# Writing y over x in six large buffers, with all transfers in a fixed order on one hardware queue

## The chip, the cores and the metric

The kernel runs on one NeuronCore of a Trainium2 chip. The metric is the time of one execution in microseconds (us), measured on the device. Every time is a median of several executions; a result is called faster or slower than the kernel before when it is clear of 2%. Smaller differences between variants are read only where the four executions of one lie apart from those of the other. Executions over 1.5% above the fastest of their kernel count as slow; ratios leave them out. Profiles come from one execution each. The "span" of a profile runs from the core's first to its last instruction; where a run lists both for one execution, the time is 1.7 to 2.2 us longer.

## The reference

```python
x: (16, 2048, 256) float32      # 32,768 rows of 1 KB
W: (256, 256);  lora_A: (256, 16);  lora_B: (16, 256);  lora_E: (16,)

y = x_flat @ W
y = y + scale * (((x_flat @ lora_A) * lora_E) @ lora_B)
```

The low-rank part can be folded into the weights, so that y = x @ weff. What remains is to read 33.55 MB of x, multiply by one 256x256 matrix and write 33.55 MB of y.

## The kernel before

Both kernels compute in the same way, two sub-rows of 128 at a time: TensorE (PE) transposes x in float32, ScalarE (ACT) casts the result to bf16, PE multiplies, VectorE (DVE) copies the product from PSUM into SBUF. What differs is where x and y lie and how the transfers are queued.

```python
CFG = dict(B_SZ=16,                       # 16 rows of 1 KB per partition: 2 MB tiles
    FIRST=[(2, [1, 1], [1, 1]), (6, [2, 4], [2, 4]), (8, [4, 4], [4, 4])],
    LAST=[(8, [4, 4], [4, 4]), (8, [8], [4, 4])],
    X_BUFS=3, Y_BUFS=3, NONSTEADY_BUFS=2, OUT_ENGINE="gpsimd", ...)   # cut

def load_x(it):                           # x tile: one of 3 buffers
    x_tile = xpool.tile([P, bsz, K], FP32, tag=f"x_{bsz}", ...)       # cut
    nc.sync.dma_start(out=x_tile[:, s:s + sz, :], in_=x_ap(it, s, s + sz))
...
for it in range(n_iters):
    y_tile = ypool.tile([P, bsz, M], FP32, tag=f"y_{bsz}", ...)       # one of 3 buffers
    for g in range(bsz // CG):
        # PE transposes -> nc.scalar.copy(out=xt, in_=psum_xt) -> PE matmuls   (cut)
        nc.vector.tensor_copy(out=y_tile[:, g * CG:(g + 1) * CG, :], in_=psum_y)
        # when a piece is complete:
        out_eng.dma_start(out=out_ap(it, s, e), in_=y_tile[:, s:e, :])
    load_x(it + 1)
```

Loads go through SyncE's hardware queue, stores through the software queue of GpSimd (POOL). A load waits until PE has read the x tile that it overwrites; DVE waits until the y tile that it overwrites has been stored.

Of the kernel before, what the change touches and what calls it, by code (L numbers as in the profile page):

```python
# [1 line left out]

# [5 lines left out]


CFG = dict(
    B_SZ=16,
    CG=2,
    IN_SPLIT=1,
    OUT_SPLIT=1,
    FIRST=[(2, [1, 1], [1, 1]), (6, [2, 4], [2, 4]), (8, [4, 4], [4, 4])],
    LAST=[(8, [4, 4], [4, 4]), (8, [8], [4, 4])],
    X_BUFS=3,
    Y_BUFS=3,
    XT_BUFS=8,  # L20
    PS_XT_BUFS=3,
    PS_Y_BUFS=3,
    NONSTEADY_BUFS=2,
    OUT_ENGINE="gpsimd",
    SETUP_ENGINE="gpsimd",
)


@with_exitstack
def kernel(  # L30
    ctx: ExitStack,
    tc: tile.TileContext,
    x: bass.AP,
    W: bass.AP,
    lora_A: bass.AP,
    lora_B: bass.AP,
    lora_E: bass.AP,
    scale: bass.AP,
    out: bass.AP,
):  # L40
    nc = tc.nc
    P = 128
    FP32 = mybir.dt.float32
    BF16 = mybir.dt.bfloat16

    CG = CFG["CG"]
    X_BUFS = CFG["X_BUFS"]
    Y_BUFS = CFG["Y_BUFS"]
    XT_BUFS = CFG["XT_BUFS"]
    PS_XT_BUFS = CFG["PS_XT_BUFS"]  # L50
    PS_Y_BUFS = CFG["PS_Y_BUFS"]

    out_eng = getattr(nc, CFG["OUT_ENGINE"])
    setup_eng = getattr(nc, CFG["SETUP_ENGINE"])

    x_flat = x.flatten_outer_dims()
    out_flat = out.flatten_outer_dims()
    N, K = x_flat.shape
    M = out_flat.shape[1]
    R = lora_B.shape[0]  # L60
    KC = K // P

    n_sub_total = N // P
    plan = []
    first = CFG["FIRST"] or []
    last = CFG["LAST"] or []
    nfirst = sum(p[0] for p in first)
    nlast = sum(p[0] for p in last)
    B_SZ = CFG["B_SZ"]
    n_mid = (n_sub_total - nfirst - nlast) // B_SZ  # L70
    assert n_mid * B_SZ + nfirst + nlast == n_sub_total, "sizes must tile exactly"
    isp = B_SZ // CFG["IN_SPLIT"]
    osp = B_SZ // CFG["OUT_SPLIT"]
    plan.extend(first)
    plan.extend([(B_SZ, [isp] * CFG["IN_SPLIT"], [osp] * CFG["OUT_SPLIT"])] * n_mid)
    plan.extend(last)
    for bsz, ip, op in plan:
        assert sum(ip) == bsz and sum(op) == bsz and bsz % CG == 0

    const = ctx.enter_context(tc.tile_pool(name="const", bufs=1))  # L80
    setup = ctx.enter_context(tc.tile_pool(name="setup", bufs=1))
    ps_setup = ctx.enter_context(tc.tile_pool(name="ps_setup", bufs=1, space=bass.MemoryType.PSUM))
    xpool = ctx.enter_context(tc.tile_pool(name="xpool", bufs=X_BUFS))
    ypool = ctx.enter_context(tc.tile_pool(name="ypool", bufs=Y_BUFS))
    xTpool = ctx.enter_context(tc.tile_pool(name="xTpool", bufs=XT_BUFS))
    ps_xT = ctx.enter_context(tc.tile_pool(name="ps_xT", bufs=PS_XT_BUFS, space=bass.MemoryType.PSUM))
    ps_y = ctx.enter_context(tc.tile_pool(name="ps_y", bufs=PS_Y_BUFS, space=bass.MemoryType.PSUM))

    row_offs = []
    acc = 0  # L90
    for bsz, _, _ in plan:
        row_offs.append(acc)
        acc += bsz * P

    def x_ap(it, s0, s1):
        bsz = plan[it][0]
        r0 = row_offs[it]
        return (
            x_flat[r0:r0 + bsz * P, :]
            .rearrange("(p b) k -> p b k", b=bsz)[:, s0:s1, :]  # L100
        )

    def out_ap(it, s0, s1):
        bsz = plan[it][0]
        r0 = row_offs[it]
        return (
            out_flat[r0:r0 + bsz * P, :]
            .rearrange("(p b) m -> p b m", b=bsz)[:, s0:s1, :]
        )

    x_tiles = {}

    steady_b = CFG["B_SZ"]

    def load_x(it):
        bsz, in_pieces, _ = plan[it]
        x_tile = xpool.tile(
            [P, bsz, K], FP32, name=f"x_tile_{bsz}", tag=f"x_{bsz}",
            bufs=X_BUFS if bsz == steady_b else CFG["NONSTEADY_BUFS"],
        )  # L120
        s = 0
        for sz in in_pieces:
            nc.sync.dma_start(out=x_tile[:, s:s + sz, :], in_=x_ap(it, s, s + sz))
            s += sz
        x_tiles[it] = x_tile

    load_x(0)

    ident = const.tile([P, P], FP32)
    make_identity(nc, ident)  # L130

    a_sb = setup.tile([P, KC, R], FP32)
    setup_eng.dma_start(out=a_sb, in_=lora_A.rearrange("(c p) r -> p c r", p=P))  # L133
    e_sb = setup.tile([R, 1], FP32)
    setup_eng.dma_start(out=e_sb, in_=lora_E[:, None])  # L135
    b_bf = setup.tile([R, M], BF16)
    nc.gpsimd.dma_start(out=b_bf, in_=lora_B)  # L137
    w_sb = setup.tile([P, KC, M], FP32)
    for c in range(KC):
        setup_eng.dma_start(out=w_sb[:, c, :], in_=W[c * P:(c + 1) * P, :])  # L140

    ps_at = ps_setup.tile([R, KC, P], FP32, name="ps_at")
    for c in range(KC):
        nc.tensor.transpose(ps_at[:, c, :], a_sb[:, c, :], ident)
    ate = setup.tile([R, KC, P], BF16)
    nc.vector.tensor_scalar(
        out=ate,
        in0=ps_at,
        scalar1=e_sb,
        scalar2=float(scale),  # L150
        op0=mybir.AluOpType.mult,
        op1=mybir.AluOpType.mult,
    )
    ps_aeb = ps_setup.tile([P, KC, M], FP32, name="ps_aeb")
    for c in range(KC):
        nc.tensor.matmul(ps_aeb[:, c, :], ate[:, c, :], b_bf, start=True, stop=True)
    weff = const.tile([P, KC, M], BF16)
    nc.vector.tensor_add(out=weff, in0=w_sb, in1=ps_aeb)  # L158

    n_iters = len(plan)  # L160
    for it in range(n_iters):
        if it not in x_tiles:
            load_x(it)
        x_tile = x_tiles.pop(it)
        bsz, _, out_pieces = plan[it]

        y_tile = ypool.tile(
            [P, bsz, M], FP32, name=f"y_tile_{bsz}", tag=f"y_{bsz}",
            bufs=Y_BUFS if bsz == steady_b else CFG["NONSTEADY_BUFS"],
        )  # L170

        bounds = []
        acc2 = 0
        for sz in out_pieces:
            acc2 += sz
            bounds.append(acc2)

        piece_idx = 0
        piece_start = 0
        for g in range(bsz // CG):  # L180
            psum_xt = ps_xT.tile([P, CG, KC, P], FP32, name="psum_xt")
            xt = xTpool.tile([P, CG, KC, P], BF16, name="xt")
            psum_y = ps_y.tile([P, CG, M], FP32, name="psum_y")
            for j in range(CG):
                sb = g * CG + j
                for c in range(KC):
                    nc.tensor.transpose(  # L187
                        psum_xt[:, j, c, :],
                        x_tile[:, sb, c * P:(c + 1) * P],
                        ident,  # L190
                    )
            nc.scalar.copy(out=xt, in_=psum_xt)  # L192
            for j in range(CG):
                for c in range(KC):
                    nc.tensor.matmul(  # L195
                        psum_y[:, j, :],
                        xt[:, j, c, :],
                        weff[:, c, :],
                        start=(c == 0),
                        stop=(c == KC - 1),  # L200
                    )
            nc.vector.tensor_copy(out=y_tile[:, g * CG:(g + 1) * CG, :], in_=psum_y)  # L202

            done = (g + 1) * CG
            while piece_idx < len(bounds) and bounds[piece_idx] <= done:
                e = bounds[piece_idx]
                s = piece_start
                out_eng.dma_start(out=out_ap(it, s, e), in_=y_tile[:, s:e, :])  # L208
                piece_start = e
                piece_idx += 1  # L210

        if it + 1 < n_iters:
            load_x(it + 1)


# [1 line left out]
_INS = ['x', 'W', 'lora_A', 'lora_B', 'lora_E', 'scale']  # L217
_OUTS = [((16, 2048, 256), 'float32')]
#: Inputs that are plain numbers.
_NUMBERS = {'scale': 1.0}  # L220


# [26 lines left out]
```

## Time and profile before

| | before |
|---|---|
| time, median (range) | 171.93 us (170.65 to 172.49) |
| span of the profile | 169.2 us |
| bytes moved, mean rate over the span | 67.55 MB, 399 GB/s |
| PE busy | 79% |

First the page of the profiled execution. Each digit is the busy share, in tenths, of one of 40 slices; PEclk is the granted PE clock, DMA the mean of the 16 DMA engines.

```profile
span 169.2 us, 2603 instructions
...
PE 134.2 (79%) x1028; PEld 104.1 (62%) x1028; DVE 84.0 (50%) x130; ACT 71.0 (42%) x129; POOL 16.5 (10%) x35
...
PE   0679999999961599962999999998969696999810
...
PEclk9999999999998589996599999999999999999975
DMA  5999999999999999999999999999999999994992
GB/s 121 310 446 430 425 408 381 435 440 422 428 419 433 440 409 438 432 420 434 430 422 434 434 430 422 426 434 434 426 434 432 434 430 422 387 426 167 379 387 108
DMA packets 6715, 67.55 MB, mean 399 GB/s; under 512 B 848, under 2 KB 1136, under 8 KB 2992
```

DMA is full almost throughout, PE is not. The rate has two weak places, the first two slices and the last four. Next, the table by stretch: start and end, length, then busy time of PE, weight loads, DVE, ACT and POOL (with counts), the granted clock, the DMA share and GB/s.

```profile
0.00:12.00 12.00, 5.53 (x24) 4.60 (x25) 0.93 (x2) 3.63 (x5) 3.64 (x11) 1.00 0.83 286
12.00:152.50 140.50, 120.35 (x941) 93.57 (x940) 76.81 (x120) 62.61 (x116) 10.16 (x19) 0.95 1.00 425
152.50:157.50 5.00, 4.77 (x41) 3.58 (x38) 3.00 (x5) 3.05 (x6) 1.07 (x2) 1.00 0.47 193
157.50:162.50 5.00, 3.53 (x29) 2.39 (x26) 3.20 (x5) 1.73 (x4) 1.07 (x2) 1.00 0.99 406
162.50:169.20 6.70, 0.00 (x0) 0.00 (x0) 0.07 (x1) 0.00 (x0) 0.53 (x1) 0.53 0.53 208
```

Look at the third row: DMA share 0.47 while PE is busy 4.77 of 5.00 us. The DMA has run out of work, and for this once PE is what everybody waits for. The timeline of POOL says what it waits for (start, duration, what, and in brackets how long POOL stood idle before and what ended it):

```profile
146.27 0.53 POOL L208 DMA_DIRECT2D out_dram<-y_tile_1523  x1 [9.19 <-DVE y_tile_1523 L202]
154.67 0.53 POOL L208 DMA_DIRECT2D out_dram<-y_tile_1631  x1 [7.87 <-DVE y_tile_1631 L202]
...
162.87 0.53 POOL L208 DMA_DIRECT2D out_dram<-y_tile_1797  x1 [1.51 <-DVE y_tile_1797 L202]
```

All loads have landed by then (the last 2 MB load was issued at 123.2 us and took 20.7), and the stores come only as fast as PE finishes tiles. In the table of waits (who waited for whom, us in total, times, longest):

```profile
PE psum_xt L187 <- DMA x_tile_657<-in_x_dram: 5.3, 1, 5.3
PE psum_xt L187 <- DMA x_tile_873<-in_x_dram: 4.6, 1, 4.6
...
DVE y_tile_551 L202 <- DMA out_dram<-y_tile_227: 3.3, 1, 3.3
```

An idle PE costs nothing at that moment, because DMA was full (436 GB/s from 52 to 58 us).

### The profile page before, as it was taken

The page shows a single profiled execution, that of the slowest core. Times are in us where ns is not written, and L with a number is a line of the kernel's source. Part 1 is how long each engine was busy: PE and PEld are TensorE (multiplying, and loading weights), DVE is VectorE, ACT ScalarE, POOL GpSimd, SP SyncE. Part 2 cuts the span into 40 slices and gives each one's busy share as a digit, 9 for nine tenths or more (in the row PEclk, how much of TensorE's full clock was granted, in tenths as well). Part 3 has the DMA queues.
Part 4 walks back from the last instruction along what each step waited for, and adds up shares of the span by engine and source line. Part 5 has one row for each costly group of instructions (what it writes and reads, how often), then busy time and mean ns, then how long its engine had stood idle before and what let it go on. Part 6 is the DMA issues. An engine that isn't in the chain of part 4 may idle for free.

```text
span 169.2 us, 2603 instructions
## 1 busy us (share of the span) xinstructions
PE 134.2 (79%) x1028; PEld 104.1 (62%) x1028; DVE 84.0 (50%) x130; ACT 71.0 (42%) x129; POOL 16.5 (10%) x35
## 2 busy tenths in 40 slices
PE   0679999999961599962999999998969696999810
PEld 0568777777741477742877777776757474777600
DVE  0027666666273066660366666665647366466620
ACT  3242555555541145530355555555535453355500
POOL 7005201010100010100101010101000010101220
PEclk9999999999998589996599999999999999999975
DMA  5999999999999999999999999999999999994992
GB/s 121 310 446 430 425 408 381 435 440 422 428 419 433 440 409 438 432 420 434 430 422 434 434 430 422 426 434 434 426 434 432 434 430 422 387 426 167 379 387 108
DMA packets 6715, 67.55 MB, mean 399 GB/s; under 512 B 848, under 2 KB 1136, under 8 KB 2992
## 3 DMA queue, kind: packets, MB, share of 16 engines
q0 software_dynamic: 3392, 33.84, 47.8%
q1 hardware_dynamic: 3312, 33.56, 47.6%
q8 instruction: 8, 0.13, 0.3%
q14 instruction: 3, 0.02, 0.0%
HBM read 33.85 MB, written 33.55 MB: 398 GB/s over the span
## 4 chain that ended last, share of the span: by engine, by line
issue 81%; POOL 9%; DMA 4%; DVE 1%; POOLq 1%; PE 0%; DVEq 0%
POOL out_dram L208 7%; DMA w_sb<-in_W_dram 4%; POOL a_sb L133 1%; PE psum_y L195 0%; DVE y_tile_106 L202 0%; DVE weff L158 0%; POOLq L244 0%; POOL w_sb L140 0%; POOL b_bf L137 0%; POOL e_sb L135 0%; POOLq L208 0%; POOL ident masks.py:199 0%; POOL ident masks.py:197 0%; POOLq masks.py:199 0%; DVEq L158 0%
## 5 line engine op out<-in xcount | busy, mean ns | idle before, releaser
L192 ACT CAST xt<-psum_xt 128x512 bf16<-128x512 f32 x128 | 69.7, 588 | 89.4 <-PE psum_xt L187 89.4
L195 PE MATMUL psum_y<-weff,xt 128*128 128x256 bf16 x512 | 72.6, 280 | 6.6 <-DVE y_tile_551 L202 1.4
L195 PEld LDWEIGHTS <-xt 128*128 128x128 bf16 x512 | 42.0, 100 | 33.5 <-ACT xt L192 27.3
L202 DVE COPY y_tile_551<-psum_y 128x512 f32<-128x512 f32 x8 | 5.1, 685 | 10.9 <-PE psum_y L195 7.6
L187 PE MATMUL psum_xt<-ident,x_tile_873 128*128 128x128 f32 x32 | 5.9, 338 | 4.6 <-DMA x_tile_873<-in_x_dram 4.6
L202 DVE COPY y_tile_767<-psum_y 128x512 f32<-128x512 f32 x8 | 5.2, 686 | 8.7 <-PE psum_y L195 8.7
L187 PE MATMUL psum_xt<-ident,x_tile_657 128*128 128x128 f32 x32 | 5.3, 315 | 5.3 <-DMA x_tile_657<-in_x_dram 5.3
L187 PEld LDWEIGHTS psum_xt<-ident,x_tile_657 128*128 128x128 f32 x32 | 4.5, 168 | 5.6 <-issue 5.5
L187 PEld LDWEIGHTS psum_xt<-ident,x_tile_873 128*128 128x128 f32 x32 | 4.9, 179 | 5.0 <-issue 4.9
L202 DVE COPY y_tile_1415<-psum_y 128x512 f32<-128x512 f32 x8 | 5.2, 688 | 4.5 <-PE psum_y L195 3.8
L202 DVE COPY y_tile_1523<-psum_y 128x512 f32<-128x512 f32 x8 | 5.2, 688 | 4.5 <-PE psum_y L195 3.8
L202 DVE COPY y_tile_1307<-psum_y 128x512 f32<-128x512 f32 x8 | 5.2, 688 | 4.5 <-PE psum_y L195 4.1
L202 DVE COPY y_tile_875<-psum_y 128x512 f32<-128x512 f32 x8 | 5.3, 688 | 3.9 <-PE psum_y L195 3.9
L202 DVE COPY y_tile_659<-psum_y 128x512 f32<-128x512 f32 x8 | 5.2, 688 | 3.5 <-PE psum_y L195 3.5
L202 DVE COPY y_tile_1199<-psum_y 128x512 f32<-128x512 f32 x8 | 5.2, 686 | 3.5 <-PE psum_y L195 3.5
L202 DVE COPY y_tile_1631<-psum_y 128x512 f32<-128x512 f32 x8 | 5.3, 688 | 3.2 <-PE psum_y L195 3.2
L202 DVE COPY y_tile_227<-psum_y 128x512 f32<-128x512 f32 x8 | 5.2, 686 | 3.1 <-PE psum_y L195 3.1
L202 DVE COPY y_tile_983<-psum_y 128x512 f32<-128x512 f32 x8 | 5.2, 686 | 3.0 <-PE psum_y L195 3.0
L202 DVE COPY y_tile_443<-psum_y 128x512 f32<-128x512 f32 x8 | 5.2, 686 | 3.0 <-PE psum_y L195 3.0
L202 DVE COPY y_tile_335<-psum_y 128x512 f32<-128x512 f32 x8 | 5.2, 686 | 3.0 <-PE psum_y L195 3.0
L202 DVE COPY y_tile_1091<-psum_y 128x512 f32<-128x512 f32 x8 | 5.2, 687 | 3.0 <-PE psum_y L195 3.0
L187 PE MATMUL psum_xt<-ident,x_tile_1521 128*128 128x128 f32 x32 | 4.3, 273 | 1.4 <-DMA x_tile_1521<-in_x_dram 1.4
(74 smaller groups left out, 143.1 us busy)
## 6 DMA issues: line engine op xcount, KB each, us to landing
x_tile_225<-in_x_dram SPq DMA_DIRECT2D x1, 2048.0 KB, 12.2
x_tile_333<-in_x_dram SPq DMA_DIRECT2D x1, 2048.0 KB, 16.9
x_tile_441<-in_x_dram SPq DMA_DIRECT2D x1, 2048.0 KB, 23.9
x_tile_549<-in_x_dram SPq DMA_DIRECT2D x1, 2048.0 KB, 14.0
out_dram<-y_tile_227 POOLq DMA_DIRECT2D x1, 2048.0 KB, 19.3
x_tile_657<-in_x_dram SPq DMA_DIRECT2D x1, 2048.0 KB, 23.0
out_dram<-y_tile_335 POOLq DMA_DIRECT2D x1, 2048.0 KB, 17.7
x_tile_765<-in_x_dram SPq DMA_DIRECT2D x1, 2048.0 KB, 22.1
```

Source lines behind the costliest of these rows:

```text
L133: setup_eng.dma_start(out=a_sb, in_=lora_A.rearrange("(c p) r -> p c r", p=P))
L187: nc.tensor.transpose(psum_xt[:, j, c, :], x_tile[:, sb, c * P:(c + 1) * P], ident,)
L192: nc.scalar.copy(out=xt, in_=psum_xt)
L195: nc.tensor.matmul(psum_y[:, j, :], xt[:, j, c, :], weff[:, c, :], start=(c == 0), stop=(c == KC - 1),)
L202: nc.vector.tensor_copy(out=y_tile[:, g * CG:(g + 1) * CG, :], in_=psum_y)
L208: out_eng.dma_start(out=out_ap(it, s, e), in_=y_tile[:, s:e, :])
```

## The change

The intent is one unbroken stream of transfers: SBUF is laid out as six buffers of one 4 MB chunk each (192 KB per partition, where the x and y tiles of before took 160 KB), y takes the place of x, and one queue carries loads and stores in a written order, loads first, so that PE is fed early and stores are always queued. Rows become 32 KB per partition. Setup tensors go on the same queue. The rest (transposes, cast, matmuls, copies) is unchanged, except that the small weight product is now in float32 and the cast has six buffers in place of eight.

```diff
-    B_SZ=16, X_BUFS=3, Y_BUFS=3, OUT_ENGINE="gpsimd", ...
+ROWS = 32
+N_CHUNKS = 8
+N_HOMES = 6
+LOAD_PIECES = {0: [8, 8, 16]}
+ORDER = [
+    "L0", "L1", "L2", "L3", "L4", "L5",
+    "S0", "S1", "L6", "S2", "L7", "S3", "S4", "S5", "S6", "S7",
+]
...
+    homes = [homes_pool.tile([P, ROWS, K], FP32, name=f"home{h}", ...) for h in range(N_HOMES)]
+    def load(c, s, e):
+        nc.sync.dma_start(out=homes[c % N_HOMES][:, s:e, :], in_=x_chunks[c, :, s:e, :])
+    def store(c, s, e):
+        nc.sync.dma_start(out=y_chunks[c, :, s:e, :], in_=homes[c % N_HOMES][:, s:e, :])
...
-            nc.vector.tensor_copy(out=y_tile[:, g * CG:(g + 1) * CG, :], in_=psum_y)
+            nc.vector.tensor_copy(out=home[:, g * CG:(g + 1) * CG, :], in_=psum_y)
...
+    done = -1
+    for step in ORDER:
+        c = int(step[1:])
+        if step[0] == "L":
+            if c:
+                for s, e in pieces(c):
+                    load(c, s, e)
+        else:
+            while done < c:
+                done += 1
+                compute(done)
+            store(c, 0, ROWS)
```

More of the change, by code (lines that the diff above doesn't have):

```diff
@@ L5 @@
 import concourse.tile as tile
-from concourse import bass_utils, mybir
+from concourse import mybir
 from concourse.masks import make_identity
 from concourse._compat import with_exitstack
-CFG = dict(
-    B_SZ=16,
-    CG=2,
-    IN_SPLIT=1,
-    OUT_SPLIT=1,
-    FIRST=[(2, [1, 1], [1, 1]), (6, [2, 4], [2, 4]), (8, [4, 4], [4, 4])],
-    LAST=[(8, [4, 4], [4, 4]), (8, [8], [4, 4])],
-    X_BUFS=3,
-    Y_BUFS=3,
-    XT_BUFS=8,
-    PS_XT_BUFS=3,
-    PS_Y_BUFS=3,
-    NONSTEADY_BUFS=2,
-    OUT_ENGINE="gpsimd",
-    SETUP_ENGINE="gpsimd",
-)
+P = 128
+FP32 = mybir.dt.float32
+BF16 = mybir.dt.bfloat16
+ROWS = 32
[6 more added lines that the diff above has]
+]
+CG = 2
 @with_exitstack
@@ L41 @@
     nc = tc.nc
-    P = 128
-    FP32 = mybir.dt.float32
-    BF16 = mybir.dt.bfloat16
-    CG = CFG["CG"]
-    X_BUFS = CFG["X_BUFS"]
-    Y_BUFS = CFG["Y_BUFS"]
-    XT_BUFS = CFG["XT_BUFS"]
-    PS_XT_BUFS = CFG["PS_XT_BUFS"]
-    PS_Y_BUFS = CFG["PS_Y_BUFS"]
-    out_eng = getattr(nc, CFG["OUT_ENGINE"])
-    setup_eng = getattr(nc, CFG["SETUP_ENGINE"])
     x_flat = x.flatten_outer_dims()
@@ L61 @@
     KC = K // P
-    n_sub_total = N // P
-    plan = []
-    first = CFG["FIRST"] or []
-    last = CFG["LAST"] or []
-    nfirst = sum(p[0] for p in first)
-    nlast = sum(p[0] for p in last)
-    B_SZ = CFG["B_SZ"]
-    n_mid = (n_sub_total - nfirst - nlast) // B_SZ
-    assert n_mid * B_SZ + nfirst + nlast == n_sub_total, "sizes must tile exactly"
-    isp = B_SZ // CFG["IN_SPLIT"]
-    osp = B_SZ // CFG["OUT_SPLIT"]
-    plan.extend(first)
-    plan.extend([(B_SZ, [isp] * CFG["IN_SPLIT"], [osp] * CFG["OUT_SPLIT"])] * n_mid)
@@ L76 @@
-    plan.extend(last)
-    for bsz, ip, op in plan:
-        assert sum(ip) == bsz and sum(op) == bsz and bsz % CG == 0
+    assert N == N_CHUNKS * ROWS * P and K == M
     const = ctx.enter_context(tc.tile_pool(name="const", bufs=1))
-    setup = ctx.enter_context(tc.tile_pool(name="setup", bufs=1))
+    homes_pool = ctx.enter_context(tc.tile_pool(name="homes", bufs=1))
+    xTpool = ctx.enter_context(tc.tile_pool(name="xTpool", bufs=6))
     ps_setup = ctx.enter_context(tc.tile_pool(name="ps_setup", bufs=1, space=bass.MemoryType.PSUM))
-    xpool = ctx.enter_context(tc.tile_pool(name="xpool", bufs=X_BUFS))
@@ L84 @@
-    ypool = ctx.enter_context(tc.tile_pool(name="ypool", bufs=Y_BUFS))
-    xTpool = ctx.enter_context(tc.tile_pool(name="xTpool", bufs=XT_BUFS))
-    ps_xT = ctx.enter_context(tc.tile_pool(name="ps_xT", bufs=PS_XT_BUFS, space=bass.MemoryType.PSUM))
-    ps_y = ctx.enter_context(tc.tile_pool(name="ps_y", bufs=PS_Y_BUFS, space=bass.MemoryType.PSUM))
-    row_offs = []
-    acc = 0
-    for bsz, _, _ in plan:
-        row_offs.append(acc)
-        acc += bsz * P
-    def x_ap(it, s0, s1):
-        bsz = plan[it][0]
-        r0 = row_offs[it]
-        return (
-            x_flat[r0:r0 + bsz * P, :]
-            .rearrange("(p b) k -> p b k", b=bsz)[:, s0:s1, :]
-        )
@@ L103, in out_ap @@
-    def out_ap(it, s0, s1):
-        bsz = plan[it][0]
-        r0 = row_offs[it]
-        return (
-            out_flat[r0:r0 + bsz * P, :]
-            .rearrange("(p b) m -> p b m", b=bsz)[:, s0:s1, :]
-        )
-    x_tiles = {}
-    steady_b = CFG["B_SZ"]
-    def load_x(it):
-        bsz, in_pieces, _ = plan[it]
-        x_tile = xpool.tile(
-            [P, bsz, K], FP32, name=f"x_tile_{bsz}", tag=f"x_{bsz}",
-            bufs=X_BUFS if bsz == steady_b else CFG["NONSTEADY_BUFS"],
-        )
-        s = 0
-        for sz in in_pieces:
-            nc.sync.dma_start(out=x_tile[:, s:s + sz, :], in_=x_ap(it, s, s + sz))
-            s += sz
-        x_tiles[it] = x_tile
@@ L127 @@
-    load_x(0)
+    ps_xT = ctx.enter_context(tc.tile_pool(name="ps_xT", bufs=3, space=bass.MemoryType.PSUM))
+    ps_y = ctx.enter_context(tc.tile_pool(name="ps_y", bufs=3, space=bass.MemoryType.PSUM))
+    x_chunks = x_flat.rearrange("(c p b) k -> c p b k", p=P, b=ROWS)
+    y_chunks = out_flat.rearrange("(c p b) m -> c p b m", p=P, b=ROWS)
+    homes = [
+        homes_pool.tile([P, ROWS, K], FP32, name=f"home{h}", tag=f"home{h}")
+        for h in range(N_HOMES)
+    ]
+    def load(c, s, e):
+        nc.sync.dma_start(out=homes[c % N_HOMES][:, s:e, :], in_=x_chunks[c, :, s:e, :])
@@ new lines, in store, with pieces @@
+    def store(c, s, e):
+        nc.sync.dma_start(out=y_chunks[c, :, s:e, :], in_=homes[c % N_HOMES][:, s:e, :])
+    def pieces(c):
+        s = 0
+        for n in LOAD_PIECES.get(c, [ROWS]):
+            yield s, s + n
+            s += n
+    first = list(pieces(0))
+    load(0, *first[0])
+    w_sb = const.tile([P, KC, M], FP32)
+    nc.sync.dma_start(out=w_sb, in_=W.rearrange("(c p) m -> p c m", p=P))
+    a_sb = const.tile([P, KC, R], FP32)
+    nc.sync.dma_start(out=a_sb, in_=lora_A.rearrange("(c p) r -> p c r", p=P))
@@ L129 @@
+    e_sb = const.tile([R, 1], FP32)
+    nc.sync.dma_start(out=e_sb, in_=lora_E[:, None])
+    b_sb = const.tile([R, M], FP32)
+    nc.sync.dma_start(out=b_sb, in_=lora_B)
+    for s, e in first[1:]:
+        load(0, s, e)
     ident = const.tile([P, P], FP32)
     make_identity(nc, ident)
-    a_sb = setup.tile([P, KC, R], FP32)
-    setup_eng.dma_start(out=a_sb, in_=lora_A.rearrange("(c p) r -> p c r", p=P))
-    e_sb = setup.tile([R, 1], FP32)
-    setup_eng.dma_start(out=e_sb, in_=lora_E[:, None])
@@ L136 @@
-    b_bf = setup.tile([R, M], BF16)
-    nc.gpsimd.dma_start(out=b_bf, in_=lora_B)
-    w_sb = setup.tile([P, KC, M], FP32)
-    for c in range(KC):
-        setup_eng.dma_start(out=w_sb[:, c, :], in_=W[c * P:(c + 1) * P, :])
     ps_at = ps_setup.tile([R, KC, P], FP32, name="ps_at")
@@ L144 @@
         nc.tensor.transpose(ps_at[:, c, :], a_sb[:, c, :], ident)
-    ate = setup.tile([R, KC, P], BF16)
+    ate = const.tile([R, KC, P], FP32)
     nc.vector.tensor_scalar(
@@ L155, with compute @@
     for c in range(KC):
-        nc.tensor.matmul(ps_aeb[:, c, :], ate[:, c, :], b_bf, start=True, stop=True)
+        nc.tensor.matmul(ps_aeb[:, c, :], ate[:, c, :], b_sb, start=True, stop=True)
     weff = const.tile([P, KC, M], BF16)
     nc.vector.tensor_add(out=weff, in0=w_sb, in1=ps_aeb)
-    n_iters = len(plan)
-    for it in range(n_iters):
-        if it not in x_tiles:
-            load_x(it)
-        x_tile = x_tiles.pop(it)
-        bsz, _, out_pieces = plan[it]
-        y_tile = ypool.tile(
-            [P, bsz, M], FP32, name=f"y_tile_{bsz}", tag=f"y_{bsz}",
-            bufs=Y_BUFS if bsz == steady_b else CFG["NONSTEADY_BUFS"],
-        )
-        bounds = []
-        acc2 = 0
-        for sz in out_pieces:
-            acc2 += sz
-            bounds.append(acc2)
-        piece_idx = 0
-        piece_start = 0
-        for g in range(bsz // CG):
+    def compute(c):
+        home = homes[c % N_HOMES]
+        for g in range(ROWS // CG):
             psum_xt = ps_xT.tile([P, CG, KC, P], FP32, name="psum_xt")
@@ L184 @@
             for j in range(CG):
-                sb = g * CG + j
-                for c in range(KC):
+                for k in range(KC):
                     nc.tensor.transpose(
-                        psum_xt[:, j, c, :],
-                        x_tile[:, sb, c * P:(c + 1) * P],
+                        psum_xt[:, j, k, :],
+                        home[:, g * CG + j, k * P:(k + 1) * P],
                         ident,
@@ L193 @@
             for j in range(CG):
-                for c in range(KC):
+                for k in range(KC):
                     nc.tensor.matmul(
                         psum_y[:, j, :],
-                        xt[:, j, c, :],
-                        weff[:, c, :],
-                        start=(c == 0),
-                        stop=(c == KC - 1),
-                    )
-            nc.vector.tensor_copy(out=y_tile[:, g * CG:(g + 1) * CG, :], in_=psum_y)
-            done = (g + 1) * CG
-            while piece_idx < len(bounds) and bounds[piece_idx] <= done:
-                e = bounds[piece_idx]
-                s = piece_start
-                out_eng.dma_start(out=out_ap(it, s, e), in_=y_tile[:, s:e, :])
-                piece_start = e
-                piece_idx += 1
-        if it + 1 < n_iters:
-            load_x(it + 1)
+                        xt[:, j, k, :],
+                        weff[:, k, :],
+                        start=(k == 0),
+                        stop=(k == KC - 1),
+                    )
+            nc.vector.tensor_copy(out=home[:, g * CG:(g + 1) * CG, :], in_=psum_y)
[11 more added lines that the diff above has]
+            store(c, 0, ROWS)
 _INS = ['x', 'W', 'lora_A', 'lora_B', 'lora_E', 'scale']
```

## The prediction

> **What bounds it now.** The DMA engines. The page counts 67.55 MB; DMA is nine tenths or more busy in 36 of 40 slices. In 10 us stretches from 60 to 140 us the stretch table reads 424 to 432 GB/s at a DMA share of 1.00. PE is busy 79%; in the timeline it works 8.2 us per 2 MB tile, against about 9.8 us in which DMA moves that tile in and out. At 52 to 58 us PE waits for x and drops to clock 0.50 while DMA stays full.
>
> Bytes flow from 2.0 to 166.2 us, mean 411 GB/s; at 428 they would need 157.8 us. So 6.4 us are lost: roughly 2 at 2 to 9 us (half-microseconds of 135 to 410 GB/s: short rows, setup tensors), about 3 at 152.5 to 155.5 us (0 to 197 GB/s: all loads are in, the next store waits for PE), the rest in gaps near 157 and 159 us and a tail of 4 KB rows near 390 GB/s. The last byte lands 3.0 us before the end.
>
> **The change.** Same bytes. Removed: y tiles, most short rows, stores from POOL (0.53 us issue each, off the critical path), loads tied to a free x tile. Moved: all transfers into one queue. DVE, ACT and PE do the same work; in the instruction order transposes do not wait for DVE, so overwriting x adds no wait.
>
> Schedule (estimate): a 4 MB chunk takes 4.19 MB/430 = 9.75 us per direction, its compute 16.4 us. Six loads end near 62 us; compute ends at about 8.5 + 16.4(n+1): 25, 41, 58, 74, 91, 107, 123, 140 us. The stores' turns begin near 62, 72, 91, 111, 121, 130, 140, 150 us: all ready, the last with 10 us to spare. Loads 6 and 7 wait for stores 0 and 1 to land, but a 4 MB transfer is always queued ahead, which hides it. Chunk 6 lands near 91, needed at 107. PE, ACT and DVE are off the critical path: one unbroken DMA stream.
>
> **Rate.** 16 KB rows go at 427 GB/s, 614 ns a row on one of 16 engines; 4 KB rows in the tail at 391, 168 ns. That gives some 20 ns per row, so 32 KB rows near 430. A mostly load-only stretch on this queue (10 to 14 us) reads 432. The Trainium skill, "DMA: Bandwidth & Descriptors", section "Issuing engines are not separate DMA queues", says transfers from different engines run on the same 16 DMA engines, so one queue should lose no bandwidth; the 432 agrees.
>
> **Sum.** 2.0 to first byte + 67.1 MB/430 = 156.0 + 1.3 for setup's small rows + 0.7 for uneven engines + 3.0 end = 163.0 us span. The timed median lies 2.5 us above the span (171.66 against 169.2): **165.5 us, 0.964 of before, range 163 to 169.5.** Faster by over 2%: 0.78; within 2%: 0.19; slower: 0.03.
>
> **Right if** DMA slices are full from the second to the last but one, none under 420 GB/s; PE works without long gaps from 9 to 140 us at clock 1.00, then idles; SyncE's waits for landed stores show no DMA gap. **Wrong if** a slice dips where load 6 or 7 waits for its store, or the last store waits for DVE.
>
> **What would make it wrong.** A pure load or pure store phase slower than the mixed one (1% of rate is 1.6 us; at 415 GB/s about 171); one slow DMA engine; compute slower than 17.6 us per chunk, which uses up the last store's slack; a stall at the beginning while setup transfers issue one by one.

## The result and the profile after

| | before | after |
|---|---|---|
| time, median (range) | 171.93 us (170.65 to 172.49) | 165.09 us (165.0 to 165.19) |
| span of the profile | 169.2 us | 163.4 us |
| PE busy | 79% | 81% |
| packets | 6715 | 3211 |

The ratio is 0.961, with an interval of 0.956 to 0.967. Ratios are the mean time of one kernel's fast runs over that of the other's in the same rounds, so they are not quite the ratio of the medians quoted. Before scattered by 1.8 us over its four executions, after by 0.2 us.

The same lines of the page:

```profile
span 163.4 us, 2576 instructions
...
PE 131.9 (81%) x1030; PEld 101.6 (62%) x1030; DVE 83.8 (51%) x130; ACT 70.3 (43%) x129; POOL 0.7 (0%) x6
...
PE   0399998999999999999999999998999899940000
...
PEclk9999999999999999999999999999999999997555
DMA  5999999998999998999999999999999999999991
GB/s 191 393 447 453 409 489 381 457 441 385 477 417 387 473 413 377 443 441 405 457 409 425 469 393 441 449 397 433 451 393 469 409 433 465 393 437 449 393 425 64
DMA packets 3211, 67.56 MB, mean 414 GB/s; under 512 B 624, under 2 KB 896, under 8 KB 896
...
PE 58%; ACT 22%; issue 5%; DMA 3%; ACTq 1%; SPq 0%; DVEq 0%; DVE 0%
```

The last line is the chain of waits by engine, to which we come back. PE now works in one block and is finished 18 us before the end. The single slices of GB/s swing between 377 and 489; one row of 32 KB takes about 1.2 us on its engine (an estimate: 431 GB/s over 16 engines). The likely reason, which was not tested, is that the trace books a row's bytes together and that many engines finish rows at about the same time: near the end, half-microseconds read from 66 to 852 GB/s. Such long rows make short slices a poor measure, and longer stretches have to be taken:

```profile
0.00:12.00 12.00, 5.16 (x19) 3.88 (x20) 1.16 (x2) 2.45 (x3) 0.70 (x6) 1.00 0.88 343
12.00:62.00 50.00, 47.67 (x374) 36.94 (x373) 29.93 (x47) 24.90 (x46) 0.00 (x0) 1.00 1.00 426
62.00:112.00 50.00, 47.92 (x392) 37.12 (x390) 31.72 (x50) 25.78 (x48) 0.00 (x0) 1.00 1.01 434
112.00:157.00 45.00, 31.13 (x253) 23.66 (x250) 21.01 (x33) 17.18 (x32) 0.00 (x0) 0.91 1.00 431
12.00:157.00 145.00, 126.73 (x1013) 97.72 (x1011) 82.66 (x128) 67.86 (x126) 0.00 (x0) 0.97 1.01 431
157.00:163.40 6.40, 0.00 (x0) 0.00 (x0) 0.00 (x0) 0.00 (x0) 0.00 (x0) 0.50 0.37 159
```

From these rows and those of before, the 5.8 us of span can be split up. In the first 12 us, 343 against 286 GB/s are 0.7 MB more, worth 1.6 us at 430 GB/s. The 62.5 MB of the stretch from 12 to 157 us would have taken 147.0 us at the 425 GB/s of before, 2.0 us more. At the end, before moved its last 4.4 MB from 152.5 to 166.2 us, which at 425 GB/s would have taken 10.4: 3.3 us were lost. After moved its last 1.02 MB from 157 to 161.0 us against 2.4: 1.6 us lost, so 1.7 us less. From the last byte to the end went 2.4 us in place of 3.0. The sum is 5.9 us, which is the 5.8 to the rounding of the rates. The medians differ by more, 6.8 us: the profiled execution of before was probably one of its faster ones.

The timeline of SyncE's queue shows the order at work:

```profile
30.11 0.34 SPq L66 DMA_DIRECT2D out_dram<-home_73  x1
46.84 0.34 SPq L66 DMA_DIRECT2D out_dram<-home_74  x1
74.51 0.34 SPq L63 DMA_DIRECT2D home_73<-in_x_dram  x1
74.94 0.79 SPq L66 DMA_DIRECT2D out_dram<-home_75  x1
...
129.27 0.33 SPq L66 DMA_DIRECT2D out_dram<-home_73  x1
146.11 0.33 SPq L66 DMA_DIRECT2D out_dram<-home_74  x1
```

Store 0 is issued at 30.1 us, when chunk 0 is done, but its turn comes only after the loads queued ahead of it: it lands at 74.4 us (44.3 us from issue to landing), and at 74.51 load 6 is let go. That wait opens no hole, since store 1 is already queued. At the other end, issue to landing in the list of transfers of the last 43 us reads:

```profile
out_dram<-home_73 SPq DMA_DIRECT2D x1, 4096.0 KB, 23.5
out_dram<-home_74 SPq DMA_DIRECT2D x1, 4096.0 KB, 16.3
```

Store 6 lands at 129.3 + 23.5 = 152.8 us, store 7 at 162.4. The last store, issued at 146.1, thus came 6.7 us before store 6 had landed. Counted in bytes it is less: 5.7 MB moved after 146.1 us, 1.5 more than store 7 itself, or 3.6 us at 431 GB/s. PE's slack is of this size, by estimate 4 to 7 us; two experiments below measure it.

### The profile page after: what moved, and what is told of

It is laid out like the page before. It is cut to its first block, busy times and chain, and to the rows that moved or that the text cites. A ratio compares the mean times of both kernels' runs of the same rounds, so it can differ in the third digit from the quotient of the medians.

```text
span 163.4 us, 2576 instructions
## 1 busy us (share of the span) xinstructions
PE 131.9 (81%) x1030; PEld 101.6 (62%) x1030; DVE 83.8 (51%) x130; ACT 70.3 (43%) x129; POOL 0.7 (0%) x6
## 2 busy tenths in 40 slices
DMA packets 3211, 67.56 MB, mean 414 GB/s; under 512 B 624, under 2 KB 896, under 8 KB 896
## 4 chain that ended last, share of the span: by engine, by line
PE 58%; ACT 22%; issue 5%; DMA 3%; ACTq 1%; SPq 0%; DVEq 0%; DVE 0%
PE psum_y L126 43%; ACT xt L123 22%; PE psum_xt L118 13%; DMA a_sb<-in_lora_A_dram 3%; PE ps_aeb L106 1%; ACTq L123 1%; DVEq L177 0%; PE ps_at L94 0%; SPq L78 0%; SPq L63 0%; DVE home_74 L133 0%
## 5 line engine op out<-in xcount | busy, mean ns | idle before, releaser
L123 ACT CAST xt<-psum_xt 128x512 bf16<-128x512 f32 x128 | 69.0, 588 | 73.5 <-PE psum_xt L118 73.4
L126 PEld LDWEIGHTS <-xt 128*128 128x128 bf16 x512 | 40.5, 99 | 34.5 <-ACT xt L123 31.0
L133 DVE COPY home_73<-psum_y 128x512 f32<-128x512 f32 x32 | 20.8, 686 | 15.3 <-PE psum_y L126 15.3
L133 DVE COPY home_74<-psum_y 128x512 f32<-128x512 f32 x32 | 20.6, 686 | 13.0 <-PE psum_y L126 13.0
L118 PE MATMUL psum_xt<-ident,home_73 128*128 128x128 f32 x128 | 19.1, 295 | 0.0
L118 PEld LDWEIGHTS psum_xt<-ident,home_73 128*128 128x128 f32 x128 | 16.4, 154 | 1.0 <-issue 0.7
L118 PE MATMUL psum_xt<-ident,home_74 128*128 128x128 f32 x128 | 16.6, 273 | 0.0
L118 PEld LDWEIGHTS psum_xt<-ident,home_74 128*128 128x128 f32 x128 | 14.5, 141 | 0.2
L133 DVE COPY home_75<-psum_y 128x512 f32<-128x512 f32 x16 | 10.3, 686 | 6.1 <-PE psum_y L126 6.1
L133 DVE COPY home_76<-psum_y 128x512 f32<-128x512 f32 x16 | 10.3, 686 | 6.1 <-PE psum_y L126 6.1
L133 DVE COPY home_77<-psum_y 128x512 f32<-128x512 f32 x16 | 10.3, 686 | 6.1 <-PE psum_y L126 6.1
L133 DVE COPY home_78<-psum_y 128x512 f32<-128x512 f32 x16 | 10.3, 686 | 6.1 <-PE psum_y L126 6.1
L118 PE MATMUL psum_xt<-ident,home_75 128*128 128x128 f32 x64 | 8.5, 273 | 0.0
L118 PE MATMUL psum_xt<-ident,home_76 128*128 128x128 f32 x64 | 8.5, 273 | 0.0
L118 PE MATMUL psum_xt<-ident,home_77 128*128 128x128 f32 x64 | 8.5, 273 | 0.0
L118 PE MATMUL psum_xt<-ident,home_78 128*128 128x128 f32 x64 | 8.5, 273 | 0.0
L118 PEld LDWEIGHTS psum_xt<-ident,home_76 128*128 128x128 f32 x64 | 7.3, 141 | 0.1
L118 PEld LDWEIGHTS psum_xt<-ident,home_78 128*128 128x128 f32 x64 | 7.3, 141 | 0.1
L118 PEld LDWEIGHTS psum_xt<-ident,home_75 128*128 128x128 f32 x64 | 7.3, 141 | 0.1
L118 PEld LDWEIGHTS psum_xt<-ident,home_77 128*128 128x128 f32 x64 | 7.3, 141 | 0.1
L94 PE MATMUL ps_at<-ident,a_sb 128*16 128x128 f32 x2 | 0.6, 394 | 6.8 <-DMA a_sb<-in_lora_A_dram 6.8
```

The costliest lines, as they stand in the source:

```text
L94: nc.tensor.transpose(ps_at[:, c, :], a_sb[:, c, :], ident)
L118: nc.tensor.transpose(psum_xt[:, j, k, :], home[:, g * CG + j, k * P:(k + 1) * P], ident,)
L126: nc.tensor.matmul(psum_y[:, j, :], xt[:, j, k, :], weff[:, k, :], start=(k == 0), stop=(k == KC - 1),)
L133: nc.vector.tensor_copy(out=home[:, g * CG:(g + 1) * CG, :], in_=psum_y)
```

## The experiments

Theory A: the gain comes from the DMA engines never running out of ready work. For that, loads must go first, so that PE finishes early and enough stores are queued while it does the last chunk. (That is its final form. As first recorded, with the run of the software queue, it also said that it does not matter which queue holds the work; that part failed, and the run with held-back stores tests what replaced it.) Rivals: B, one hardware queue (or not mixing loads and stores) is what helps; C, the six buffers and writing in place are what help; and the length of the rows. The changed kernel was run again as a yardstick with the first two sets.

### The yardstick, twice

> The changed kernel itself again, as the yardstick for the runs beside it. All theories: 165.0 to 165.3 us, span near 163.4.

> The changed kernel again, the yardstick of this set: 165.0 to 165.5 us.

Measured: 165.34 us and 165.25 us. The kernel before, on the same chip, took 173.09 and 173.05 us in its fast executions (173.13 and 173.09 with one slow one of 174.8).

### Stores back on the software queue

```diff
-        nc.sync.dma_start(out=y_chunks[c, :, s:e, :], in_=homes[c % N_HOMES][:, s:e, :])
+        nc.gpsimd.dma_start(out=y_chunks[c, :, s:e, :], in_=homes[c % N_HOMES][:, s:e, :])
```

> Only the stores move back to the software queue of POOL; buffers, row size and in-place writing stay. Theory A (the gain is that the 16 DMA engines never run out of ready work, and it does not matter which queue holds it): 165 to 166.5 us; stores start near 31 us beside the loads, about 3 to 5 us of stores are still waiting when the last one is issued near 146 us. Theory B (the gain comes from the single hardware queue, or from not mixing loads and stores): 168 us or more, and a lower rate in the stretches where both queues run.

Measured: 168.17 us (168.04 to 170.07), 2.8 us over the yardstick. The number under A was missed, and so was its claim that the queue does not matter; B's number was met. But look at how it got there. The profiled execution was the slowest of the four (170.07 us), so only its pattern is used. PE's timeline shows three waits that the changed kernel does not have:

```profile
95.26 0.41 PE L118 MATMUL psum_xt<-ident,home 128*128 128x128 f32 x2 [1.82 <-DMA home<-in_x_dram]
114.89 0.66 PE L118 MATMUL psum_xt<-ident,home 128*128 128x128 f32 x2 [3.36 <-DMA home<-in_x_dram]
135.41 0.66 PE L118 MATMUL psum_xt<-ident,home 128*128 128x128 f32 x2 [2.88 <-DMA home<-in_x_dram]
```

The last store was issued at 155.6 us, not 146.1, and before it the DMA was mostly idle, with a share of 0.26 (stretch table, columns as above):

```profile
150.00:155.50 5.50, 4.05 (x34) 2.88 (x31) 3.75 (x6) 2.15 (x4) 0.00 (x0) 1.00 0.26 110
```

The Trainium skill, "DMA: Bandwidth & Descriptors", section "Queues, rings and completion order", says that each DMA engine round-robins between the queue rows it has work for, at packet granularity. The trace fits. From 62 to 112 us the two queues moved (packets, MB, share of the engines' time):

```profile
q0 software_dynamic: 360, 10.72, 51.1%
q1 hardware_dynamic: 359, 10.42, 49.0%
```

And from 97.7 to 138.8 us, when PE had used up the chunks loaded ahead, stores were issued 20.5 us apart, about twice the 9.75 us that a 4 MB transfer takes alone, against 16.4 us when PE sets the pace. Loads lost half of the DMA to stores that nobody needed yet. That is a reason for the loss, but it does not yet exclude B.

### Stores on the software queue, but held back until the loads are ahead

```diff
+            if c == 0:
+                gate = const.tile([1, 1], FP32)
+                nc.gpsimd.tensor_scalar(out=gate, in0=homes[4][0:1, 0, 0:1],
+                    scalar1=0.0, scalar2=None, op0=mybir.AluOpType.mult)
+                one = homes[0][0:1, 0, 0:1]
+                nc.gpsimd.tensor_add(out=one, in0=one, in1=gate)
+                last = store(c, 0, ROWS)
+            else:
+                with tc.issue_after(getattr(last, "ins", last)):
+                    last = store(c, 0, ROWS)
```

> Stores on the software queue as in the earlier run, but the first store must wait until load 4 has landed (a one-element add of zero to its data that reads load 4), and the others follow in order. Theory A1 (the earlier run lost its 3 us because stores on a second queue take half of the DMA from the loads, so that PE starved and issued the last store 9 us later): loads come first again, PE works without a gap, the last store is issued near 146 us, 165 to 166.5 us. Theory B1 (the software queue itself is slower): 168 us or more again.

Measured: 165.77 us (165.63 to 165.92), 0.5 us over the yardstick; the result is still correct. The software queue is back, and nearly all of the loss is gone. POOL's timeline and the stretch table:

```profile
128.44 0.53 POOL L66 DMA_DIRECT2D out_dram<-home  x1 [15.87 <-DVE home L133]
144.84 0.53 POOL L66 DMA_DIRECT2D out_dram<-home  x1 [15.87 <-DVE home L133]
```

```profile
12.00:157.00 145.00, 126.04 (x1013) 97.05 (x1011) 82.68 (x128) 67.80 (x126) 4.89 (x10) 0.97 1.01 431
```

The last store is issued at 144.8 us, and the rate is the 431 GB/s of the single hardware queue. B falls as the main cause: the queue matters because its fixed order puts loads first. What the remaining 0.5 us are was not followed up.

### The last load later in the order, by three places and by two

```diff
-    "S0", "S1", "L6", "S2", "L7", "S3", "S4", "S5", "S6", "S7",
+    "S0", "S1", "L6", "S2", "S3", "S4", "S5", "L7", "S6", "S7",     # first run
+    "S0", "S1", "L6", "S2", "S3", "S4", "L7", "S5", "S6", "S7",     # second run
```

> Same kernel, only the order changes: the last load goes behind stores 3, 4 and 5. Bytes, rows, queue and buffers are the same. Theory A (what counts is that stores are still queued while PE works on the last chunk): the last load lands near 143 us instead of 113, PE waits from about 129 us and comes back with a cold clock, the last store is issued near 161 to 163 us, the DMA stands still for 8 to 11 us after 152 us, total 173.5 to 178 us. Theory B (long rows and one hardware queue): 165 us, unchanged.

Measured: 176.04 us (175.71 to 176.38), 10.7 us over the yardstick; its ratio to the kernel before is 1.019. Bytes, rows, queue and buffers are those of the changed kernel; only the position of one load differs. PE's timeline, then the stretch table:

```profile
142.89 1.97 PE L118 MATMUL psum_xt<-ident,home 128*128 128x128 f32 x8 [15.31 <-DMA home<-in_x_dram]
```

```profile
150.00:163.00 13.00, 10.96 (x89) 8.02 (x86) 7.89 (x13) 6.10 (x12) 0.00 (x0) 1.00 0.01 4
```

For 13 us the DMA moves 4 GB/s while PE does the last chunk. PE had waited 15.3 us, its granted clock had dropped to 0.50 (142 to 145 us), and the first eight transposes took 1.97 us where the same group takes 1.04. The Trainium skill, "TensorE: Matmul & The Clock Gate", section "Part 1: The HAM clock gate (the "warmup" mystery)", gives a half clock for an idle array and about 3.4 us of work to be rid of it; this trace agrees with the half clock. The granted clock averages 0.58 from 145 to 148 us and 1.00 after that, so that the return took some 4.6 us of work, an estimate.

> The last load goes behind stores 3 and 4, two places later than in the changed kernel and one earlier than in the run that put it behind store 5. By 9.75 us per transfer it lands near 132.5 us, 3 to 4 us after PE is done with chunk 6; the last chunk then ends near 150 us, and the last store is issued at about 150 to 151.5 us, just when store 6 runs out near 151. If the slack of about 5 us read from the trace is real, the total moves by 0 to 1.5 us only: 165.2 to 166.8 us. If any later load costs in proportion (10.8 us for three places in the other run), 169 us or more.

Measured: 166.42 us (166.03 to 166.98). There was no yardstick in this set; against 165.25 of the one before it is 1.2 us (against 165.37 of the last variant below, from its own set and as fast as the yardstick, 1.1 us). PE waited 5.7 us for the load, the last store was issued near 152.6 us, and the hole is short:

```profile
133.21 1.97 PE L118 MATMUL psum_xt<-ident,home 128*128 128x128 f32 x8 [5.68 <-DMA home<-in_x_dram]
```

```profile
150.00:152.00 2.00, 1.47 (x12) 0.76 (x10) 1.24 (x3) 1.07 (x2) 0.00 (x0) 1.00 0.16 66
```

So 6.5 us of delay in the last store cost 1.2 us, and about 16.5 us cost 10.7: the first 5 to 6 us are free. This is inside the 4 to 7 us read from the trace. It also says how to read the chain of waits of the changed kernel, which puts 58% of the span down to PE: that chain follows instructions and does not see the queue of transfers. PE was not what the kernel waited for.

### In place undone: three x buffers and three y buffers

```diff
-N_HOMES = 6
+N_HOMES = 3          # and three "outs" of the same size, into which DVE copies
-    "L0", "L1", "L2", "L3", "L4", "L5",
-    "S0", "S1", "L6", "S2", "L7", "S3", "S4", "S5", "S6", "S7",
+    "L0", "L1", "L2", "S0", "L3", "S1", "L4", "S2", "L5", "S3", "L6",
+    "S4", "L7", "S5", "S6", "S7",
```

> In place undone: three 32 KB buffers for x and three for y in place of six shared ones, one queue, loads only three chunks ahead (L0 L1 L2 S0 L3 S1 L4 ...). Theory A: by the same count of 9.75 us per transfer and 16.8 us of compute per chunk every store is still ready at its turn or up to 1 us late, so 165 to 167.5 us: writing y over x and loading six ahead are not needed in themselves. Theory C (six chunks of look-ahead are what gains): 169 us or more, with DMA gaps before stores 1 to 3.

Measured: 166.4 us (165.62 to 168.64). The execution of 168.64 was slow; the other three have a median of 166.34, 1.0 us over the yardstick. PE waited 4.6 us in all for loads and the last store was issued near 152.5 us, with a short hole between 147 and 157 us, as in the run just told (118 GB/s from 150 to 152.5 us). Theory C falls as the main cause. Six shared buffers buy the slack; three and three in a good order get within about 1 us.

### More x buffers in the kernel before

```diff
-    X_BUFS=3, NONSTEADY_BUFS=2,
+    X_BUFS=6, NONSTEADY_BUFS=1,      # first run
+    X_BUFS=5, NONSTEADY_BUFS=2,      # second run
```

> The kernel before with six x buffers of 16 KB in place of three (and one each of the small tiles, to make room); nothing else. Theory A (before lost its time at the end because its loads were held back by free buffers and PE was left with work when the stores ran dry): loads run ahead, PE stands still less than before, the last store is issued earlier than 162.9 us and the hole of 3 us at 152 to 156 us shrinks to under 1.5 us: 167.5 to 170 us. If buffers do not matter: 171.5 to 173 us as before.

Measured: 182.12 us, 5% slower than before. Part of it was my own doing: with one buffer for each small tile, the last two tiles waited for each other, and POOL stood 12.2 us before the last but one store. The run could not tell the theories apart, so it was mended.

> The kernel before with five x buffers for three, small tiles left at two (the run with six had to cut those to one, and its last two tiles then waited for each other). If look-ahead buffers for x alone mend the end: 167.5 to 170 us. If, as the waits of the run with six say (30.7 us of DVE waiting for stores to leave the three y tiles), the stores lose half of the DMA to the loads and PE is then held back by y: 171.5 to 174 us, no gain, and the hole before the last 2 MB store stays.

Measured: 171.74 us (171.07 to 172.15), the same as before in its set (171.78 us with two slow executions, 171.18 without; ratio 1.005, interval 0.998 to 1.012). Waits:

```profile
DVE y_tile L202 <- DMA out_dram<-y_tile: 30.7, 7, 10.3
```

More look-ahead for x only moves the wait: loads and stores still share the DMA, stores fall behind, and PE is held up by y tiles that have not left. The last 2 MB store went out at 155.4 us, as late as before (154.7 us).

### The kernel before with its stores on the hardware queue

```diff
-    OUT_ENGINE="gpsimd",
+    OUT_ENGINE="sync",
```

> The kernel before with its stores on the hardware queue of the loads, in the order that the scheduler gives, without the changed kernel's order. If one hardware queue is what gains: 165 to 169 us. If the order on it is what counts: SyncE stands before stores whose tile PE has not finished while loads could run (the load of the fourth 2 MB tile is issued near 44 us instead of 25), the DMA has holes, 180 us or more.

Measured: 208.02 us, 22% slower. SyncE stood 175.0 us in total before stores that DVE had not yet filled, and the loads behind them could not be issued; the load of the fourth 2 MB tile went out near 46 us in place of 25.6. One queue alone is a loss here; it becomes a gain with an order in which an entry that waits has enough work queued ahead of it.

### Shorter rows

```diff
-        for n in LOAD_PIECES.get(c, [ROWS]):
+        for n in LOAD_PIECES.get(c, [ROWS // 2, ROWS // 2]):
-            store(c, 0, ROWS)
+            store(c, 0, ROWS // 2)
+            store(c, ROWS // 2, ROWS)
```

> Every 4 MB transfer is issued as two of 2 MB, so a row is 16 KB instead of 32 KB; order, queue and buffers stay. If a row costs some 20 ns beyond its bytes, as the prediction worked out from 4 KB and 16 KB rows, about 2,000 more rows on 16 engines cost 2.5 us: 167.5 to 168 us. If the stretch rates of the two traces are the measure (428 against 431 GB/s), 0.9 us: about 166 us, less up to 0.6 us because the engines can finish closer together. If long rows are what gained most of the 6.6 us: 169 us or more.

Measured: 166.33 us (166.17 to 166.51), 1.1 us over the yardstick. The stretch from 12 to 157 us:

```profile
12.00:157.00 145.00, 126.28 (x1012) 97.41 (x1010) 82.69 (x128) 67.76 (x126) 0.00 (x0) 0.97 1.01 427
```

So 427 against 431 GB/s. The run had 5371 packets against 3211; 2,160 more (240 of them under 512 B: the edit also doubles the number of transfers) on 16 engines for 1.1 us are 8 ns each, not the 20 ns that the prediction took from the tail of before. This is an estimate: of the 1.1 us some 0.4 lie outside the span (time minus span is 2.2 us here, 1.8 in the yardstick), while the two rates alone would make it 1.4 us over the stretch, or 10 ns. Long rows are worth about 1.1 of the 6.8 us.

### The last store in four pieces

```diff
-            store(c, 0, ROWS)
+            n = 8 if c == N_CHUNKS - 1 else ROWS
+            for s in range(0, ROWS, n):
+                store(c, s, s + n)
```

> Only the last store is cut into four of 8 KB rows. If the ragged end (the engines finish over some 2 us) comes from the length of the last rows, 164.4 to 164.9 us. If the engines are apart by work done earlier, no gain: 165.0 to 165.6 us, the shorter rows costing up to 0.4 us.

Measured: 165.37 us (165.24 to 165.5). No gain: bytes still trickle from 159 to 161.5 us. This fits engines that are already apart when the last store begins, but that was not seen directly, and what would set them apart is open.

No variant beat the changed kernel.

## Why the prediction was right

**Bound by the DMA: right.** The changed kernel moves the same bytes in one stream, and the runs that lost most show holes in that stream (110 GB/s for 5.5 us with the stores on the software queue, 4 GB/s for 13 us with the last load latest). (One count is off: the page before has 37 slices at nine tenths or more, not 36.)

**Time: 165.09 us against 165.5.** The terms of the sum compare like this:

| term, us | predicted | measured |
|---|---|---|
| first byte | 2.0 | about 1.5 |
| stream of x and y | 156.0 (at 430 GB/s) | 155.7 (at 431 GB/s) |
| small rows and setup bytes | 1.3 | about 2.0 (0.45 MB of other bytes, 1.0, and 1.0 lost in the first 12 us) |
| ragged end | 0.7 | 1.6 |
| after the last byte | 3.0 | 2.4 |
| time minus span | 2.5 | 1.7 |

The ragged end and the small rows were sized too small; the three fixed terms too large. The last of these set the median of three executions against the span of one; in the runs that list both for one execution of before, the difference is 1.7 to 1.9 us. The errors nearly cancel, so the closeness of the total is partly luck. The mechanism is not.

**Rate: right figure, wrong derivation.** 431 GB/s were measured for 430. The cost per row of 20 ns behind it was taken from a tail in which stores came one by one; the run with 16 KB rows gives about 8 ns. The Trainium skill, "HBM Reference", section "Specifications (TRN2)", puts a core streaming alone at about 425 GB/s, bounded by its 16 DMA engines; over 145 us this case shows 431 with 32 KB rows, 427 with 16 KB rows.

**"One queue should lose no bandwidth": right but half the story.** With loads ahead, two queues carry 431 GB/s as well. What the second queue costs is priority: 2.8 us when stores may compete from the start, 0.5 us when they are held back.

**Schedule: right in order, off in size.** Every store was ready at its turn, and the waits of loads 6 and 7 opened no hole. But chunks ended later than predicted, the last at about 146 us, not 140, and the slack was about 5 us, not 10. Most of it is the start. The prediction counts the first chunk from 8.5 us, but PE began its y matmuls at 12.0 us: lora_A was queued behind the first 1 MB of x and PE waited for it until 6.8 us, and the float32 weight product took 2 us. (Before had begun no earlier, at 12.3 us.) The first chunk then took 18.1 us: until about 16.4 us, eight matmuls took 1.9 us where they take 1.1 later, although the granted clock reads 1.00 there. Of the other seven chunks four took 16.4 us as predicted and three 16.7 to 16.8; the gated run shows 16.4 at its last four stores, and the cause of this small difference was not followed up.

**A sign that was badly chosen:** "none under 420 GB/s" for single slices. They swing from 377 to 489, in a stream that has no hole. By the letter of it this sign failed.

**Open:** why before scatters by several us between executions (170.1 to 174.8) while the changed kernel repeats within 0.4; why the stretches of the ungated software-queue run (422 GB/s from 33 to 147 us) were some 2% slower than the gated one's, which is one profile each; the cause of the ragged end; and whether the small gains add up, as no variant undid rows and separate buffers together.

## What to carry to other kernels

When the DMA is the bound and still 4% of its time is missing, look for the stretch in which PE is busy and the DMA is not; here it was at the end, and its cause was an earlier stretch in which PE starved without harm. Let loads go ahead of stores, so that more store time is queued when the last load lands than the last piece of compute takes; a written order on one queue did this here, a gate in front of the stores did nearly as well, and more x buffers or one queue alone did not. Measure the slack by moving one transfer: the delay that costs nothing is the slack.

## What the Trainium skill lacked or had wrong

- "DMA: Bandwidth & Descriptors", in its rules for kernel authors, says that spreading DMAs over issuing engines only saves sequencer time. The rule lacks what follows from the page's own paragraph on arbitration: stores on a second queue take half of the DMA from loads that are more urgent. Here the two queues moved 10.72 and 10.42 MB from 62 to 112 us, chunks came 20.5 us apart where PE needs 16.4, and the time was 168.2 us against 165.8 with the same queues and the stores held back.
- The same page has no measured cost of a row among rows of many KB; what it says per packet is about small transfers. Halving 32 KB rows to 16 KB cost 1.1 us for 2,160 more packets, by estimate about 8 ns each on its engine.
- "HBM Reference" has about 425 GB/s for a core streaming alone; 431 GB/s were held for 145 us here, 99% of the 435 GB/s that "DMA: Bandwidth & Descriptors" gives as the ceiling.
- No page warns that GB/s over short slices misleads with long rows: slices of 4.1 us read 377 to 489 GB/s in a stream that averaged 431.
